# Splitting the blocks of U ahead of the V loop: an adding DMA for every second block, VectorE for the rest

## The chip, the core and the metric

One core of a Trainium2 chip. It has five engines, each with an instruction queue of its own that is worked off in order: TensorE (PE, with its weight loads PEld shown apart), VectorE (DVE), ScalarE (ACT), GpSimd (POOL) and SyncE (SP), which here only issues DMAs. SP's transfers are the hardware queue q1 in the profile, GpSimd's the software queue q0; both run on the same 16 DMA engines. The metric is the device time of one execution in microseconds (us).

## The reference, cut to what matters

A decoder layer for 512 tokens of width 1024: attention in two head groups, then PEER. PEER routes each token to 128 of 16384 single-neuron experts (8 heads, 16 each), and for the chosen ones computes

```python
expert = jnp.take_along_axis(cand_i, best_pos, axis=-1)
g = jax.nn.softmax(best_s, axis=-1)
act = jax.nn.gelu(jnp.einsum('cd,chkd->chk', hc, u[expert]), approximate=False)
out = jnp.einsum('chk,chkd->cd', g * act, v[expert])
```

## The kernel before, in words

For the first 384 tokens (three tiles of 128) PEER is done densely: U and V are cut into 128 blocks of 128 experts; all activations of a block are computed and multiplied by a gate matrix that is zero where an expert was not chosen. The last 128 tokens gather their rows of U and V by indirect DMA on GpSimd's queue instead.

Every float32 product is made of three matmuls on rounded halves: a matrix is split in a high part (`hi`, rounded) and a low part (`lo = raw - hi`), and `mm3` (lines 147 to 150) multiplies high by high, high by low and low by high. `u_block(b)` (line 875) does this for one block of U: SP loads 512 KB of float32 (`raw`, two buffers, L878), ScalarE writes `hi` (L881, three buffers), the low part is made in one of three ways (below, three buffers), then 24 matmuls (8 chunks of three; L148, L149, L150) fill one PSUM bank (`p_u`), and ScalarE takes the GELU of it (L892). The activations of the first 22 blocks are stored to DRAM by SP (`a_d`, two buffers, L894).

The low part is made

- by an adding DMA where `b in UDMA`: ScalarE writes the negated rounded copy into `lo` (L883), and GpSimd issues a DMA that reads the block from DRAM once more and adds it (L884);
- else by GpSimd where `b in UPOOL`, else by VectorE, as one subtraction of two tiles (L886).

`UDMA` is asked first, so that of `UPOOL`'s 14 numbers only 0 and 52 count; blocks 1, 2, 3, 53, 54 and 55 are VectorE's, and so are blocks 56 to 127.

```python
if b in UDMA:
    nc.scalar.activation(lo, raw, AF.Copy, scale=-1.0)
    nc.gpsimd.dma_start(lo.rearrange("p k e -> p (k e)"), ut[b], accum_op=ALU.add)
else:
    (nc.gpsimd if b in UPOOL else nc.vector).tensor_tensor(lo, raw, hi.bitcast(F32), op=ALU.subtract)
```

56 blocks (`NAHEAD`) are done ahead, while the gates are made. Routing (`route`: 8 largest values, replace, indices, all on VectorE), the choice of experts (`choose`: VectorE, with ScalarE's expanded copies `ix`, L776), `spread`, and then for each of the three token tiles eight steps: `hot` writes one-hot tables on VectorE (L823, L826, two buffers each), `gates` multiplies them on PE (32 small matmuls a step, `p_g`, L842), ScalarE copies the result (`st`, L845), and SP stores 1 MB (`g_d`, L848). After each step `u_ahead(2)` adds two blocks of U; six come before the first step and two after the last. Routing and choice for the next tiles are written between the steps of tiles 0 and 1. In the text the first gathers (`gu`, L918, on GpSimd's queue, with L926 on VectorE) stand in the second half of tile 2.

Then the loop over V (`v_load`, `v_mm`): per block two loads, two splittings, 18 matmuls (L1019), and one block of U for the later blocks, plus the gathers for the last 128 tokens.

The order of each engine's instructions is not the order of the text: a planner under the kernel runs the program against costs of its own and takes what is ready, the most urgent first. `tc.high_priority(offset=UPRI)` makes the load and splitting of a U block as urgent as text 1000 instructions earlier. The order it finds is then fixed, and on the chip every engine keeps to it.

Of the kernel before, what the change touches and what calls it, by code (L numbers as in the profile page):

```python
# [53 lines left out]
XAT = (0, 1)  # L54
UPRI = 1000
PACE = 1.02
UPOOL = tuple(range(0, 56, 4))
LAST = 4
UDMA = tuple(range(4, 52))
VRB = 3  # L60
ARB = 3
RATE = (0.2, 2.75, 1.1)
# [13 lines left out]
def hybrid_layer(ctx: ExitStack, tc, x, pos, wada, wada_n, cols, w_small, w_in_a, w_in_b, wuk, wuv,  # L76
# [798 lines left out]
    def u_block(b, psum):  # L875
        with tc.high_priority(offset=UPRI):
# [4 lines left out]
            nc.scalar.activation(hi, raw, AF.Copy)  # L881
# [5 lines that stand above are left out]
        o = psum(f"p_u{b}")[:, :DT]  # L887
# [247 lines left out]
```

## Time and profile before

| | us |
|---|---|
| median of 3 timed runs | 1613.36 (1611.5 to 1625.25) |
| the profiled execution | 1609.18 |
| its span, first to last instruction | 1607.1 |
| around the span | 2.1 |

The profile is of one execution. A window of it is named by microseconds from the start of the span. The attention part ends near 430 us, the gates and the blocks of U ahead take from there to about 760 us, and the loop over V and the end take the rest.

### The profile page before, as it was taken

The page shows a single profiled execution, that of the slowest core. Times are in us where ns is not written, and L with a number is a line of the kernel's source. Part 1 is how long each engine was busy: PE and PEld are TensorE (multiplying, and loading weights), DVE is VectorE, ACT ScalarE, POOL GpSimd, SP SyncE. Part 2 cuts the span into 40 slices and gives each one's busy share as a digit, 9 for nine tenths or more (in the row PEclk, how much of TensorE's full clock was granted, in tenths as well). Part 3 has the DMA queues.
Part 4 walks back from the last instruction along what each step waited for, and adds up shares of the span by engine and source line. Part 5 has one row for each costly group of instructions (what it writes and reads, how often), then busy time and mean ns, then how long its engine had stood idle before and what let it go on. Part 6 is the DMA issues. An engine that isn't in the chain of part 4 may idle for free.

```text
span 1607.1 us, 23098 instructions
## 1 busy us (share of the span) xinstructions
PE 1503.8 (94%) x8136; PEld 1319.1 (82%) x8138; DVE 1230.5 (77%) x2623; ACT 753.6 (47%) x1190; POOL 538.8 (34%) x439
## 2 busy tenths in 40 slices
PE   6888898999899888899999999999999999999997
PEld 5757687777788788789888999999999999998885
DVE  7698986856989798343567887888888888776886
ACT  4655446544268678586333333333333333333333
POOL 2323213112111222111003645554555555553420
PEclk7999899999999999999999999999999999999999
DMA  8233333513199999998987999999999999997974
GB/s 341 79 118 106 106 131 105 171 66 96 29 239 275 295 303 289 304 287 258 316 283 263 342 388 348 323 364 309 345 355 326 342 324 355 348 306 252 334 254 156
DMA packets 161733, 410.93 MB, mean 256 GB/s; under 512 B 12865, under 2 KB 69073, under 8 KB 158289
## 3 DMA queue, kind: packets, MB, share of 16 engines
q1 hardware_dynamic: 116832, 248.81, 45.6%
q0 software_dynamic: 43776, 159.40, 30.5%
q8 instruction: 64, 1.05, 0.3%
q10 hardware_dynamic: 1008, 1.24, 0.2%
q14 instruction: 53, 0.43, 0.1%
HBM read 375.71 MB, written 33.69 MB: 255 GB/s over the span
## 4 chain that ended last, share of the span: by engine, by line
PE 69%; DVE 10%; ACT 8%; DMA 7%; issue 5%; POOL 1%; DVEq 0%; POOLq 0%; ACTq 0%; SPq 0%
PE acc L1019 31%; PE p_u L150 8%; PE p_u L149 8%; PE p_u L148 8%; PE po L561 2%; DMA a_d<-a 2%; DMA ulo<-in_ut_dram 2%; ACT st L845 2%; PE p_g L842 1%; PE p_b L148 1%; PE tp L551 1%; ACT ulo L883 1%; PE pl L535 1%; PE p_b L150 1%; PE p_b L149 1%
## 5 line engine op out<-in xcount | busy, mean ns | idle before, releaser
L150 PE MATMUL p_u<-h,ulo 128*128 128x384 f32 x1024 | 349.0, 341 | 17.1 <-DMA ulo<-in_ut_dram 17.1
L148 PE MATMUL p_u<-h,uhi 128*128 128x384 f32 x1024 | 348.6, 340 | 3.0 <-ACT a L892 3.0
L149 PE MATMUL p_u<-h,uhi 128*128 128x384 f32 x1024 | 346.3, 338 | 0.0
L918 POOL DMA_INDIRECT gu<-in_un_dram,e x128 | 190.2, 1486 | 270.1 <-DVE gu L926 239.2
L881 ACT ACTIVATE uhi<-u 128x1024 fp32r<-128x1024 f32 x128 | 135.5, 1060 | 265.8 <-PE p_u L149 213.5
L918 POOL DMA_INDIRECT gv<-in_pv_dram,e x128 | 189.4, 1479 | 187.2 <-DVE acc L937 156.3
L1019 PE MATMUL acc<-vhi,wh 128*128 128x512 f32 x768 | 237.2, 389 | 0.6 <-ACT wh L1011 0.6
L1019 PE MATMUL acc<-vlo,wh 128*128 128x512 f32 x768 | 237.3, 389 | 0.0
L1019 PE MATMUL acc<-vhi,wl 128*128 128x512 f32 x768 | 237.1, 389 | 0.0
L150 PEld LDWEIGHTS p_u<-h,ulo 128*128 128x128 f32 x1024 | 193.7, 189 | 21.7 <-DMA ulo<-in_ut_dram 19.0
L1011 ACT ACTIVATE wh<-w 128x384 fp32r<-128x384 f32 x128 | 67.3, 525 | 302.8 <-issue 179.5
L148 PEld LDWEIGHTS p_u<-h,uhi 128*128 128x128 f32 x1024 | 193.8, 189 | 7.1 <-ACT a L892 4.0
L149 PEld LDWEIGHTS p_u<-h,uhi 128*128 128x128 f32 x1024 | 193.8, 189 | 2.9
L1012 DVE TENSOR_TENSOR wl<-w,wh 128x384 fp32r<-128x384 f32 x128 | 71.4, 558 | 136.6 <-ACT wh L1011 136.4
L926 DVE SCALAR_TENSOR_TENSOR gu<-gu,h2n 128x1024 f32<-128x1024 f32 x128 | 154.2, 1221 | 21.3 <-DMA gu<-in_un_dram,e 21.1
L1019 PEld LDWEIGHTS acc<-vlo,wh 128*128 128x128 f32 x768 | 144.0, 188 | 30.3 <-DVE vlo L998 0.4
L1019 PEld LDWEIGHTS acc<-vhi,wl 128*128 128x128 f32 x768 | 144.2, 188 | 30.1
L937 DVE SCALAR_TENSOR_TENSOR acc<-gv,w,acc 128x1024 f32<-128x1024 f32 x127 | 162.6, 1280 | 5.0 <-DMA gv<-in_pv_dram,e 4.9
L1019 PEld LDWEIGHTS acc<-vhi,wh 128*128 128x128 f32 x768 | 143.2, 188 | 25.4 <-ACT wh L1011 0.9
L998 DVE TENSOR_TENSOR vlo<-v,vhi 128x1024 fp32r<-128x1024 f32 x128 | 156.2, 1220 | 3.9 <-ACT vhi L997 3.8
L997 ACT ACTIVATE vhi<-v 128x1024 fp32r<-128x1024 f32 x128 | 135.5, 1058 | 10.3 <-PE acc L1019 4.3
L884 POOL DMA_DIRECT2D ulo<-in_ut_dram x48 | 42.5, 886 | 208.9 <-ACT ulo L883 202.4
(356 smaller groups left out, 2460.2 us busy)
## 6 DMA issues: line engine op xcount, KB each, us to landing
u<-in_ut_dram SPq DMA_DIRECT2D x128, 512.0 KB, 6.3
v<-in_pv_dram SPq DMA_DIRECT2D x128, 512.0 KB, 4.9
ulo<-in_ut_dram POOLq DMA_DIRECT2D x48, 512.0 KB, 8.3
g_d<-st SPq DMA_DIRECT2D x24, 1024.0 KB, 7.4
gt<-g_d SPq DMA_DIRECT2D x48, 512.0 KB, 8.5
wada<-in_wada_dram SPq DMA_DIRECT2D x32, 512.0 KB, 3.3
raw_b<-in_w_in_b_dram SPq DMA_DIRECT2D x12, 512.0 KB, 3.7
a_d<-a SPq DMA_DIRECT2D x22, 192.0 KB, 7.3
```

Of the source, the lines that this page charges most:

```text
L148: nc.tensor.matmul(o, ahi, bhi, start=start, stop=False, **kw)
L149: nc.tensor.matmul(o, ahi, blo, start=False, stop=False, **kw)
L150: nc.tensor.matmul(o, alo, bhi, start=False, stop=stop, **kw)
L881: nc.scalar.activation(hi, raw, AF.Copy)
L918: nc.gpsimd.indirect_dma_start(out=t, out_offset=None, in_=src, in_offset=bass.IndirectOffsetOnAxis(ap=e0[:, s:s + 1], axis=0))
L926: nc.vector.scalar_tensor_tensor(t, t, 1.0, h2n, op0=ALU.mult, op1=ALU.mult, accum_out=dot0[:, s:s + 1])
L937: nc.vector.scalar_tensor_tensor(acc0, t, w0[:, s:s + 1], acc0, op0=ALU.mult, op1=ALU.add)
L997: nc.scalar.activation(hi, raw, AF.Copy)
L998: nc.vector.tensor_tensor(lo, raw, hi.bitcast(F32), op=ALU.subtract)
L1011: nc.scalar.activation(wh, w, AF.Copy)
L1012: last[0] = nc.vector.tensor_tensor(wl, w, wh.bitcast(F32), op=ALU.subtract).ins
L1019: nc.tensor.matmul(accs[2 * j + n], l[:, js], r[:, n * 512:(n + 1) * 512], start=b == 0 and i == 0, stop=b == NK - 1 and i == 2)
```

## The change

The numbers of the blocks change hands; no instruction is new.

```diff
-UPOOL = tuple(range(0, 56, 4))
+UPOOL = ()
 LAST = 4
-UDMA = tuple(range(4, 52))
+UDMA = tuple(range(5, 53, 2))
```

The adding DMA keeps the 24 odd blocks from 5 to 51. The 24 even blocks from 4 to 50 go from it to VectorE, and so do blocks 0 and 52 from GpSimd.

## Rows read from the trace of the kernel before

**Rows 1.** The head of the page: span, and busy time with share of the span and number of instructions of each engine.

```profile
span 1607.1 us, 23098 instructions
...
PE 1503.8 (94%) x8136; PEld 1319.1 (82%) x8138; DVE 1230.5 (77%) x2623; ACT 753.6 (47%) x1190; POOL 538.8 (34%) x439
```

**Rows 2.** Busy time by stretch. Columns: stretch in us from the span's start, its length, then busy us (and number of instructions) of PE, of PE's weight loads, of VectorE, of ScalarE and of GpSimd, the granted clock of TensorE, the busy share of the DMA engines, GB/s. The seventh row is the whole of the first five and the 33 us before them; the last row is the loop over V.

```profile
480.00:530.00 50.00, 46.95 (x342) 43.78 (x342) 48.48 (x216) 40.87 (x48) 11.65 (x15) 1.00 0.97 278
530.00:545.00 15.00, 10.39 (x56) 9.46 (x54) 7.83 (x45) 4.85 (x7) 2.37 (x3) 0.77 1.05 315
545.00:585.00 40.00, 35.62 (x290) 32.66 (x289) 35.47 (x107) 36.85 (x45) 8.50 (x9) 1.00 1.01 303
585.00:640.00 55.00, 48.88 (x373) 45.01 (x372) 47.51 (x161) 45.56 (x55) 13.38 (x15) 1.00 0.98 278
640.00:690.00 50.00, 42.12 (x307) 38.68 (x306) 20.70 (x34) 30.86 (x39) 10.00 (x11) 0.97 1.00 291
690.00:745.00 55.00, 52.77 (x404) 50.83 (x403) 20.72 (x31) 42.04 (x51) 10.48 (x10) 1.00 1.01 295
...
447.00:690.00 243.00, 213.56 (x1525) 197.65 (x1524) 188.36 (x711) 181.45 (x219) 52.88 (x60) 0.98 0.99 281
...
870.00:1572.00 702.00, 702.00 (x3491) 632.54 (x3490) 576.91 (x725) 250.69 (x345) 353.75 (x236) 1.00 0.93 329
```

**Rows 3.** The same view for the instructions on the PSUM tile of the gate products (p_g) alone; columns: stretch, length, PE, ScalarE, clock, DMA share, GB/s.

```profile
447.00:690.00 243.00, 42.25 (x576) 67.59 (x72) 0.98 0.99 281
690.00:745.00 55.00, 10.84 (x160) 19.66 (x22) 1.00 1.01 295
```

**Rows 4.** The same for the U products (p_u); columns: stretch, length, PE, PE's weight loads, ScalarE, clock, DMA share, GB/s.

```profile
447.00:690.00 243.00, 179.55 (x913) 159.25 (x912) 18.54 (x38) 0.98 0.99 281
690.00:745.00 55.00, 44.64 (x244) 41.65 (x243) 4.72 (x10) 1.00 1.01 295
```

**Rows 5.** What PE waited for from 690 to 745 us. Columns: who waited, for whom, us in total, times, longest us.

```profile
PE p_g L842 <- ACT st L845: 2.2, 5, 0.5
```

**Rows 6.** The busy time by stretch for the score products of the routing (p_sc); columns: stretch, length, PE, weight loads, VectorE, clock, DMA share, GB/s.

```profile
447.00:690.00 243.00, 6.15 (x24) 4.22 (x24) 27.53 (x150) 0.98 0.99 281
```

**Rows 7.** What PE waited for from 447 to 690 us, columns as in rows 5.

```profile
PE p_u L150 <- DMA ulo<-in_ut_dram: 17.1, 11, 3.7
PE p_g L842 <- ACT st L845: 6.5, 11, 1.5
PE p_g L842 <- DVE oh L826: 3.5, 3, 1.4
PE p_u L148 <- ACT a L892: 1.7, 2, 0.9
```

**Rows 8.** The chain that ended last, from 505 to 550 us: start us, us, what.

```profile
522.46 9.86 DMA a_d<-a
...
532.92 10.02 DMA a_d<-a
```

**Rows 9.** ScalarE's wait for the store of the activations in the same stretch, columns as in rows 5.

```profile
ACT a L892 <- DMA a_d<-a: 12.5, 5, 5.0
```

**Rows 10.** VectorE's four longest waits in the same stretch, columns as in rows 5.

```profile
DVE o L811 <- ACT tt L805: 21.1, 2, 19.9
DVE oh L823 <- PE p_g L842: 11.4, 5, 7.2
DVE gu L926 <- DMA gu<-in_un_dram,e: 10.0, 3, 4.8
DVE eq L780 <- ACT ix L776: 8.0, 5, 2.6
```

**Rows 11.** The DMA view from 447 to 690 us: queue, packets, MB and the share of the 16 engines' time in the stretch; then issues: tile, queue, kind, number, KB each, median us from issue to landing.

```profile
q0 software_dynamic: 7390, 26.93, 51.2%
q1 hardware_dynamic: 10837, 41.20, 47.4%
...
ulo<-in_ut_dram POOLq DMA_DIRECT2D x39, 512.0 KB, 8.4
...
gu<-in_un_dram,e POOLq DMA_INDIRECT x13, 11.9
```

**Rows 12.** The GpSimd queue's row of the same view from 900 to 1400 us, where that queue issues gathers only.

```profile
q0 software_dynamic: 25983, 94.58, 50.3%
```

**Rows 13.** The instructions that write the low part (tile ulo), whole kernel. Columns: line, engine, kind, number, ns min/median/max, first and last start in us, shape.

```profile
L886 DVE TENSOR_TENSOR ulo<-u,uhi x78: 1207/1222/1229, 435.2 to 1433.5; 128x1024 fp32r<-128x1024 f32 x78
L883 ACT ACTIVATE ulo<-u x48: 1039/1043/1096, 445.6 to 736.1; 128x1024 fp32r<-128x1024 f32 x48
L884 POOL DMA_DIRECT2D ulo<-in_ut_dram x48: 854/858/1130, 447.0 to 737.5; - x48
L886 POOL TENSOR_TENSOR ulo<-u,uhi x2: 2342/2567/2792, 429.6 to 740.5; 128x1024 fp32r<-128x1024 f32 x2
```

**Rows 14.** The chain that ended last, in one even step of the last gates: start us, us, what.

```profile
718.49 1.03 ACT ulo L883
719.52 0.38 ACT a L892
719.89 0.95 ACT st L845
```

**Rows 15.** VectorE's wait for ScalarE before a low part, 690 to 780 us, columns as in rows 5.

```profile
DVE ulo L886 <- ACT uhi L881: 18.3, 6, 5.6
```

## The prediction, made before the changed kernel ran

> **What bounds the kernel now.** I read the head of the page first [rows 1]: PE is busy for 94% of the span, but that is a mean over stages with different limits. The table of stretches comes next [rows 2]. Its last row, the loop over V, has PE busy for all of 702 us: nothing that happens beside PE can shorten it, and it holds no block that the change touches. So the change is worth what it does between 430 and 760 us, where U ahead and the gates share the chip.
>
> In that stage two paces stand side by side. From 690 to 745 us the gates run evenly: 5 steps (160 gate matmuls at 32 a step [rows 3]) and 10.2 blocks of U (244 matmuls at 24 a block [rows 4]) in 55 us, 11.0 us a step, with PE waiting for 2.2 us [rows 5]. That is PE's own pace. From 447 to 690 us there are 38.0 blocks (913/24 [rows 4]) and 18 steps (576/32 [rows 3]), and 6.2 us of score products [rows 6]. At the even pace the blocks and steps would take 18 x 11.0 = 198 us and the two blocks over that some 8 us (PE needs 44.6/10.2 = 4.4 us a block [rows 4]); with the score products 212 us. They took 243. So some 31 us lie there, and no more: this is the ceiling of any gain in that stretch.
>
> Who holds PE there: the adding DMA 17.1 us, ScalarE's copies and GELUs 6.5 + 1.7 us, VectorE's tables 3.5 us [rows 7]; some 29 us. After such waits the granted clock is 0.77 of full speed from 530 to 545 us and 0.97 from 640 to 690 (a mean over its two levels, 2.4 and 1.2 GHz) [rows 2], which adds 0.23 x 15 + 0.03 x 50 = 5 us. And behind two of these waits stands the DMA too: the chain goes through two stores of activations of 9.9 and 10.0 us [rows 8], for which ScalarE stood for 12.5 us [rows 9], with its copies for the U blocks queued behind. The DMA engines are busy for 99% of the stretch, VectorE for 188.4 us of 243 [rows 2], with 54.6 us idle, nearly all in four waits [rows 10].
>
> **What the change takes from the DMA engines.** The GpSimd queue took 51.2% of 243 us, 124 us, for 39 adding DMAs and 13 gathers [rows 11]. What a gather costs alone is seen in the loop over V: 50.3% of 500 us for 94.6 MB, 2.66 us a MB [rows 12], 1.39 us for its 0.524 MB. 13 gathers are 18 us, so 39 adds are 106 us, 2.7 us each; a plain load on the hardware queue is 0.474 x 243/41.2 = 2.80 us a MB [rows 11], 1.5 us. Half of the adds, 20 in the stretch, free 20 x 2.7 = 54 us: the engines' load goes from 240 to about 186 us of 243, 77%.
>
> The Trainium skill ("DMA: Bandwidth & Descriptors", section "SDMA does more than copy") says that a DMA engine's arithmetic lies in line with the data stream, and gives no rate. Taken as a plain load's price, half the adds would free 29 us and leave the engines at 87%; the trace has 2.7 us for an add against 1.5, so the measurement decides, and the relief is the larger one.
>
> **What it takes from ScalarE and GpSimd.** 24 negated copies of 1.043 us and 24 issues of 0.858 us [rows 13], 25 and 21 us. In the even steps a negated copy stands ahead of the GELU and of the gate copy that PE waits for [rows 14]; one of two per step goes. Blocks 0 and 52: 2.34 and 2.79 us on GpSimd become 1.22 on VectorE [rows 13]; I take 0, with 1.6 us as the bound of either sign each, since VectorE is full at the first and PE has blocks in hand at the second.
>
> **What comes back to PE.** Half of the blocks lose the wait for the adding DMA (8.5 of 17.1 us); the other half's adds land sooner, and fewer of them stand between GpSimd's gathers. I take 11 us, between 8.5 and 17.1. Of the 8.2 us on ScalarE I take 4 (bounds 0 and 8.2), of the clock 3 (0 and 5), of the even steps 2 (0 and 2.2). Sum: 20 us off; all bounds together give 33, and the ceiling above with the even steps gives the same 33.
>
> **What it adds.** 26 subtractions of 1.222 us on VectorE [rows 13], 31.8 us; 20 of them in 447 to 690, 24.4 us against 54.6 us idle. But 21.1 us of that idle time is the start of a tile's gates, nearly all one wait of 19.9 us [rows 10] late in the stretch, which takes no work that is due earlier. From 480 to 640 VectorE is busy for 139.3 of 160 us [rows 2], and its share there, 12 subtractions, is 15 us into 20.7. Queued behind each of them stand the one-hot tables for PE's gate products and the routing of the next tile, and the block's `raw` buffer, so SP's next load, waits for it as well. PE meanwhile has U blocks to do. I take 9 us as lost: between 0 (PE always has another block) and 25.6 (20 in the stretch and one in the full VectorE before it, each delaying PE by its length). Half-way down, because VectorE is full in one part of the stretch (97% from 480 to 530) and not in the other. No price is in the trace for the new order that the planner will find; it acts through the same waits, and I leave it inside these bounds.
>
> So the stage gets shorter by 20 - 9 = 11 us: 1598 us against the profiled 1609.2, which lies 4 us below the median; on the median's footing **1602 us**. By its terms' likelier ends this case runs from 4 to 19 us off, 1594 to 1609.
>
> **Rivals.**
> 1. The whole relief. The subtractions fit into VectorE's idle time because the waits for gathers (10.0 us) and for PE (11.4 us) [rows 10], which slow DMAs and a late PE cause, go. Then 25 us off (19 to 33): 1588. For it: the DMA engines at 99%, and 54.6 us idle against 24.4. Against it: VectorE at 97% from 480 to 530.
> 2. VectorE becomes the bound of tiles 0 and 1. All 25.6 us show: -20 + 25.6 = +5, no change to be measured, 1619. For it: 139.3 of 160 us. Against: PE doesn't depend on the gates alone, it has U blocks as well.
> 3. Slower, by one mechanism: VectorE's queue is in order, and a subtraction waits there for `hi`, which ScalarE writes when PE gives a buffer back. VectorE, which could run ahead of PE until now, is then tied to it. Where such waits are seen, they are 18.3/6 = 3.05 us [rows 15]. 20 of these are 61 us; with 24.4 of work 85.4 against 54.6 idle: 31 us slower, 1644. It decides from (54.6 - 24.4)/20 = 1.5 us a subtraction; at 2.3 us it costs the 16 us that are 1%. For it: the planner's times are not the chip's. Against: the six waits lie where VectorE has nothing else to do, and three buffers of `hi` leave two blocks, 8 us, of lead.
>
> **How the numbers follow.** Forecast 0.48, rival 1 0.22, rival 2 0.17, rival 3 0.13. A measurement tells about 1%, 16 us, from no change. Faster by more: rival 1 and the forecast's far end, 0.30. Slower by more: most of rival 3, 0.09. Within: 0.61. Range 1586 (27 us off, some 0.07 beyond) to 1623 (10 us more, some 0.12 beyond). Both signs hold chance; the likeliest case's own range is 1594 to 1609.
>
> **What would show it.** Right: 24 negated copies and 24 adds, 104 subtractions on VectorE and none on GpSimd; the DMA share between 447 and 690 near 0.8; PE's wait for the adding DMA under 7 us; the stores of activations landing in well under 9.9 us and ScalarE's wait for them under 4; the loop over V as long as before, beginning some 11 us earlier; VectorE over 93% busy from 480 to 640. Wrong: PE's waits for VectorE's tables or low parts of more than 10 us (rival 2), waits of VectorE for `hi` of more than 1.5 us a block (rival 3), or a DMA share still at 0.99.

## The result and the profile after

The changed kernel took 1602.83 us in the median of 12 runs, the kernel before 1620.69 in its 12 runs. The ratio on record, which is not the quotient of these two medians (0.9890), is 0.9912 with a 95% interval of 0.9885 to 0.9940, some 14 us of 1613 (10 to 19). The profiled execution took 1602.78 us. Its head, beside [rows 1]:

```profile
span 1600.3 us, 23058 instructions
...
PE 1501.5 (94%) x8136; PEld 1318.7 (82%) x8138; DVE 1257.0 (79%) x2649; ACT 731.7 (46%) x1166; POOL 516.6 (32%) x413
```

VectorE is 26.5 us busier, ScalarE 21.9 and GpSimd 22.2 less. The low parts, beside [rows 13]:

```profile
L886 DVE TENSOR_TENSOR ulo<-u,uhi x104: 1205/1218/1289, 435.8 to 1424.7; 128x1024 fp32r<-128x1024 f32 x104
L883 ACT ACTIVATE ulo<-u x24: 1037/1041/1078, 451.7 to 726.0; 128x1024 fp32r<-128x1024 f32 x24
L884 POOL DMA_DIRECT2D ulo<-in_ut_dram x24: 864/871/1134, 453.4 to 727.3; - x24
```

The table of stretches, columns and order as in [rows 2] (the whole stretch from 447 to 690 us first); the last row is the loop over V, which now begins some 10 us earlier:

```profile
447.00:690.00 243.00, 223.78 (x1617) 210.70 (x1615) 219.16 (x770) 173.70 (x211) 37.75 (x41) 0.98 0.85 256
480.00:530.00 50.00, 47.44 (x347) 44.49 (x346) 47.98 (x185) 37.69 (x46) 4.16 (x6) 1.00 0.79 233
530.00:545.00 15.00, 12.53 (x64) 12.21 (x63) 13.14 (x68) 6.40 (x9) 5.79 (x7) 0.89 1.02 346
545.00:585.00 40.00, 37.57 (x294) 34.78 (x293) 36.41 (x117) 34.63 (x42) 4.48 (x5) 1.00 0.80 230
585.00:640.00 55.00, 51.82 (x405) 48.89 (x404) 52.47 (x177) 41.87 (x51) 7.41 (x9) 1.00 0.84 263
640.00:690.00 50.00, 43.59 (x349) 40.22 (x347) 37.84 (x63) 34.63 (x43) 12.36 (x11) 0.97 0.95 303
690.00:745.00 55.00, 52.16 (x401) 50.26 (x401) 22.84 (x32) 36.49 (x45) 3.52 (x4) 1.00 0.78 235
860.00:1562.00 702.00, 701.88 (x3490) 632.24 (x3489) 576.70 (x726) 250.06 (x343) 355.88 (x236) 1.00 0.93 329
```

The reader is to see three things. The loop over V is as full as before: nothing came from there. The DMA engines fell from 99% to 85% of the stretch. And VectorE was filled where it had idled: 37.8 of 50 us from 640 to 690 (20.7 before), and from 480 to 640 the four rows add up to 150.0 of 160 (139.3 before). PE paid little for it: its wait for VectorE's tables grew from 3.5 to 7.8 us. What PE waited for from 447 to 690 us, beside [rows 7]:

```profile
PE p_g L842 <- DVE oh L826: 7.8, 11, 1.4
PE p_u L150 <- DMA ulo<-in_ut_dram: 7.7, 3, 3.2
PE p_g L842 <- ACT st L845: 3.4, 6, 1.0
```

VectorE's waits there, beside [rows 10]; the waits of 21.1 us for `tt` and 11.4 us for PE's gates are gone:

```profile
DVE ulo L886 <- ACT uhi L881: 15.1, 11, 4.0
DVE gu L926 <- DMA gu<-in_un_dram,e: 6.6, 2, 3.8
DVE eq L780 <- ACT ix L776: 1.3, 2, 1.1
```

The DMA view of the stretch, beside [rows 11]. ScalarE's wait for `a_d`, 12.5 us in [rows 9], has no row any more:

```profile
q1 hardware_dynamic: 11536, 44.57, 53.6%
q0 software_dynamic: 4738, 17.28, 30.8%
...
ulo<-in_ut_dram POOLq DMA_DIRECT2D x20, 512.0 KB, 7.9
a_d<-a SPq DMA_DIRECT2D x21, 192.0 KB, 5.8
gu<-in_un_dram,e POOLq DMA_INDIRECT x13, 9.0
```

**The stage as one account.** From ScalarE's last copy of `qT` to PE's first product of the loop over V (L1019) PE has the same work in both kernels, 2175 rows. So the stage's length is PE's busy time plus its waits (a microsecond or so lies in gaps that no wait is listed for). The same table, the kernel before first:

```profile
427.93:775.23 347.30, 309.12 (x2175) 289.79 (x2175) 237.88 (x863) 246.10 (x297) 67.52 (x73) 0.98 0.95 275
```

and the changed kernel:

```profile
430.35:764.85 334.50, 306.75 (x2175) 290.32 (x2175) 264.42 (x890) 224.49 (x272) 42.02 (x47) 0.97 0.82 248
```

12.8 us less, of 14 in the timed runs. PE's clock has two levels, 2.4 and 1.2 GHz, and the waits do not show what the lower one costs. In the changed kernel the lower one was granted from 462.15 to 465.57 us, just behind a wait of 2.1 us for an adding DMA; columns as in [rows 2]:

```profile
462.15:465.57 3.42, 3.42 (x13) 3.42 (x12) 3.39 (x31) 0.89 (x2) 0.10 (x1) 0.50 0.86 206
```

The products of U in it start every 0.32 us, and those behind it every 0.17 (start us, us, what):

```profile
464.26 0.53 PE L150 MATMUL p_u<-h,ulo 128*128 128x384 f32 x1
464.58 0.53 PE L148 MATMUL p_u<-h,uhi 128*128 128x384 f32 x1
...
467.30 0.33 PE L149 MATMUL p_u<-h,uhi 128*128 128x384 f32 x1
467.47 0.33 PE L150 MATMUL p_u<-h,ulo 128*128 128x384 f32 x1
```

So the stretch at 1.2 GHz costs 0.15 of each 0.32 us that PE is busy in it. The waits over this stage, the time in it that PE was busy at 1.2 GHz, and the same of every kernel run later (us; "adds" are adding DMAs in the stage; the last column but one is an estimate, the stage less 0.15/0.32 of the column before it; the timed ratio is against the kernel before):

| kernel | adds | stage | PE <- adding DMA | PE <- ScalarE (`st`, `a`) | PE <- VectorE's tables | PE busy at 1.2 GHz | stage without its cost | timed ratio |
|---|---|---|---|---|---|---|---|---|
| before | 48 | 347.3 | 17.1 | 12.3 | 3.5 | 12.1 | 342 | 1 |
| changed | 24 | 334.5 | 7.7 | 7.5 | 7.8 | 14.0 | 328 | 0.9912 |
| e1_plain_even | 24 and 24 plain | 345.1 | 12.3 | 13.4 | 3.5 | 18.4 | 336 | 0.9971 |
| e2_upool_only | 48 | 351.4 | 18.1 | 11.9 | 3.5 | 22.1 | 341 | 0.9995 |
| e3_udma_only | 24 | 343.6 | 13.4 | 7.7 | 7.5 | 13.1 | 337 | 0.9978 |
| e4_act_copy | 24 | 340.9 | 10.6 | 9.8 | 6.2 | 16.0 | 333 | 0.9957 |
| e5_no_low | 24 | 355.5 | 0.8 | 32.0 | 3.6 | 27.6 | 343 | 1.0028 |
| e6_dve_and_dma | 48 | 353.6 | 16.6 | 12.7 | 4.1 | 23.1 | 343 | 1.0032 |
| e7_pool0 | 24 | 337.9 | 8.5 | 10.3 | 5.5 | 19.1 | 329 | 0.9944 |
| e8_tile0_dma | 33 | 344.9 | 14.3 | 10.3 | 6.3 | 16.2 | 337 | 0.9980 |
| e9_short_sub | 24 | 341.0 | 9.4 | 7.6 | 10.4 | 16.7 | 333 | 0.9953 |
| e10_double_sub | 24 | 335.9 | 8.8 | 12.3 | 5.5 | 10.6 | 331 | 0.9946 |
| e11_all_dve | 0 | 327.6 | 0 | 7.1 | 8.9 | 10.7 | 323 | 0.9880 |
| e12_third | 32 | 345.8 | 11.5 | 13.1 | 3.3 | 27.8 | 333 | 0.9993 |

The stage's difference over 1609 us agrees with each timed ratio within 0.3%, so the stage carries the effect as far as these times can tell; 0.3% is some 5 us, a third of it. (The span doesn't serve: the last copy of `qT`, ahead of all that is changed, lay anywhere from 428 to 440 us in the profiled executions, and what follows the stage took 831.9 us before, 835.5 in the changed kernel and 832.6 to 836.2 in the others. So the two profiled executions as wholes are only 6.4 us apart.) Each row is of one execution, and how much the stage varies from one execution to the next was not measured.

With the estimated cost of 1.2 GHz taken out the stages fall into an order that the plain lengths hide: 341 to 343 us for the three kernels with 48 adds, 328 to 333 with 24 and VectorE on the other blocks, 323 without any.

### The profile page after: what moved, and what is told of

It reads as the page before. It is cut to its first block, busy times and chain, and to the rows that moved or that the text cites. A ratio compares the mean times of both kernels' runs of the same rounds, so it can differ in the third digit from the quotient of the medians.

```text
span 1600.3 us, 23058 instructions
## 1 busy us (share of the span) xinstructions
PE 1501.5 (94%) x8136; PEld 1318.7 (82%) x8138; DVE 1257.0 (79%) x2649; ACT 731.7 (46%) x1166; POOL 516.6 (32%) x413
## 4 chain that ended last, share of the span: by engine, by line
PE 64%; DVE 10%; ACT 6%; issue 5%; DMA 4%; POOL 1%; SPq 0%; DVEq 0%; POOLq 0%; ACTq 0%
PE acc L1019 28%; PE p_u L150 8%; PE p_u L148 8%; PE p_u L149 8%; ACT st L845 2%; PE po L561 2%; DMA gu<-in_un_dram,e 1%; DMA ulo<-in_ut_dram 1%; DVE ulo L886 1%; PE p_g L842 1%; ACT uhi L881 1%; PE pl L535 1%; PE tp L551 1%; PE p_b L148 1%; PE p_b L149 1%
## 5 line engine op out<-in xcount | busy, mean ns | idle before, releaser
L918 POOL DMA_INDIRECT gv<-in_pv_dram,e x128 | 193.9, 1515 | 181.4 <-DVE acc L937 148.9
L1019 PE MATMUL acc<-vlo,wh 128*128 128x512 f32 x768 | 237.3, 389 | 0.9 <-DVE vlo L998 0.9
L1019 PE MATMUL acc<-vhi,wh 128*128 128x512 f32 x768 | 237.4, 390 | 0.4 <-ACT wh L1011 0.2
L1019 PE MATMUL acc<-vhi,wl 128*128 128x512 f32 x768 | 237.1, 389 | 0.0
L886 DVE TENSOR_TENSOR ulo<-u,uhi 128x1024 fp32r<-128x1024 f32 x104 | 126.9, 1220 | 63.9 <-ACT uhi L881 63.6
L1019 PEld LDWEIGHTS acc<-vlo,wh 128*128 128x128 f32 x768 | 144.0, 188 | 31.4 <-DVE vlo L998 1.6
L1019 PEld LDWEIGHTS acc<-vhi,wl 128*128 128x128 f32 x768 | 144.1, 188 | 30.1
L1019 PEld LDWEIGHTS acc<-vhi,wh 128*128 128x128 f32 x768 | 143.1, 188 | 25.6 <-ACT wh L1011 1.0
```

Of the source, the lines that this page charges most:

```text
L918: nc.gpsimd.indirect_dma_start(out=t, out_offset=None, in_=src, in_offset=bass.IndirectOffsetOnAxis(ap=e0[:, s:s + 1], axis=0))
L1019: nc.tensor.matmul(accs[2 * j + n], l[:, js], r[:, n * 512:(n + 1) * 512], start=b == 0 and i == 0, stop=b == NK - 1 and i == 2)
```

## The experiments

All were timed against the kernel before. The theory was that of the prediction: the DMA engines' relief and ScalarE's give, VectorE's subtractions cost. Nearly every edit makes the planner find a new order; e1 is the exception, there every engine keeps the order of before (e2 comes near it). The diffs of e1, e2, e3 and e6 are against the kernel before, the others against the changed one.

**e1_plain_even.** The DMA engines' arithmetic alone.

```diff
-    nc.gpsimd.dma_start(..., ut[b], accum_op=ALU.add)
+    nc.gpsimd.dma_start(..., ut[b], **(dict(accum_op=ALU.add) if b % 2 else {}))
```

> The kernel before, but for the even blocks 4 to 50 the DMA that adds is a plain DMA of the same bytes on the same queue (the low part is then the raw block; that part of the computation is wrong). The order of every engine's instructions is the same as before, and nothing else changes: only the price of 24 transfers, 2.7 us of the DMA engines by the trace, falls to that of a plain one, some 1.5. My theory (the gain is relief of the DMA engines): 24 x 1.2 = 29 us of DMA time go, about half of what the change frees, so 6 to 12 us faster than before (ratio 0.992 to 0.996), PE's wait for the adding DMA from 17 to 10 us or less, ScalarE's wait for the stores of activations from 12.5 to under 8. Rival A (the gain is ScalarE's relief from the negated copies) and rival B (the gain is the planner's new order): no change, 0.999 to 1.001.

Measured: ratio 0.9971 (0.9944 to 0.9997), some 5 us, short of the expected 0.992 to 0.996, which the interval reaches; it leaves out 1, though only just. PE's wait for the adding DMA fell from 17.1 to 12.3 us and ScalarE's for the stores of activations from 12.5 to 10.3, both less than expected. The two main queues from 447 to 690 us, as in [rows 11]:

```profile
q1 hardware_dynamic: 11134, 42.50, 50.1%
q0 software_dynamic: 7488, 27.27, 41.9%
```

Nearly the same bytes (27.27 MB, 26.93 before) took 41.9% and not 51.2% of the engines. 41.9% of 243 us less 18 for the gathers is 84 us for 39 transfers; with half of them adds of 2.7 us, a plain one comes to 1.6 us. The Trainium skill ("DMA: Bandwidth & Descriptors", section "SDMA does more than copy") places the arithmetic in line with the stream and gives no rate; on this queue the same 512 KB cost 1.1 us more with it. So the price of an add in the prediction holds, and arithmetic is the smaller part of the gain, some 5 of 14 us: the block still waits for its DMA.

**e2_upool_only.** Blocks 0 and 52 alone.

```diff
-UPOOL = tuple(range(0, 56, 4))
+UPOOL = ()
```

> One part of the change alone: blocks 0 and 52 go from GpSimd to VectorE, the adding DMA keeps blocks 4 to 51. My prediction took 0 for this part, with 1.6 us per block as the bound of either sign: ratio 0.998 to 1.002. Rival from the trace after: at the start VectorE is full, the low part of block 0 waits in its queue, the raw buffer comes free 5 us later and with it the next load, so PE begins the blocks 2 to 4 us later: 1.001 to 1.0025, and the third load of U is issued near 437 us in place of 432.

Measured: 0.9995 (0.9968 to 1.0021). The term of 0 holds within this interval, which does not exclude the lower half of the rival's range: the next load of U was issued at 437.5 us and not at 432.0, and the one stage that was profiled is 4.1 us longer.

**e3_udma_only.** The other line alone. With the even blocks out of `UDMA`, `UPOOL` counts again and GpSimd makes the low part of 14 blocks (0, 4, 8 to 52).

```diff
-UDMA = tuple(range(4, 52))
+UDMA = tuple(range(5, 53, 2))
```

> The other part alone: the adding DMA keeps the odd blocks 5 to 51, and GpSimd keeps its list, so that blocks 0, 4, 8 to 52 are subtracted on GpSimd (14, of 2.6 us each), the other even ones on VectorE. If VectorE's added work is what is lost (my 9 us), half of it comes back: 3 to 6 us faster than the change (ratio to before 0.986 to 0.990), VectorE busy for some 140 us of 480 to 640 in place of 150. Rival: the subtractions on GpSimd hold up the adds and gathers behind them on its queue and take twice as long: slower than the change, 0.993 to 1.000, with PE's wait for low parts above 12 us.

Measured: 0.9978 (0.9955 to 1.0001), the rival's range. So the empty `UPOOL` is not idle text: most of the gain hangs on it, 0.22% being left of 0.88. The stage is 9.1 us longer than the changed kernel's. PE's wait for the adding DMA is 5.7 us more of that, and 3.9 us are waits for the transposes of `spread` (`tp_s`, L803) behind VectorE, which the changed kernel does not have. One thing that stands ahead of these transposes is seen in the trace. GpSimd's longest subtraction (the median is 2.45 us), columns start us, us, what:

```profile
574.75 6.26 POOL L886 TENSOR_TENSOR ulo<-u,uhi 128x1024 fp32r<-128x1024 f32 x1 [3.77 <-ACT uhi L881]
```

and VectorE beside it:

```profile
578.33 0.29 DVE L782 TENSOR_TENSOR eq<-eq 128x256 f16<-128x256 f16 x1
578.53 0.23 DVE L796 CAST i<-sel 128x128 int32<-128x128 f32 x1
578.67 2.43 DVE L782 TENSOR_TENSOR eq<-eq 128x128 f16<-128x128 f16 x1
```

GpSimd stands while VectorE runs eight two-input operations in a row, until these break off at a CAST; then VectorE's next one, half the size of one of 0.29 us, takes 2.43 us and ends as GpSimd ends, at 581.0. Each holds the other up. The Trainium skill ("SBUF — State Buffer", section "SBUF: two separate sides") says that the two share a pair of ports as an exclusive lock for a whole instruction; these rows agree, on both sides. Of the 14 subtractions only one other was held up by more than half a microsecond (4.00 us). So this accounts for a few us, and why the adds were waited for longer, by the lock, by GpSimd's queue or by the planner's order, is not shown.

**e4_act_copy.** The changed kernel with ScalarE's relief taken back.

```diff
 else:
+    if b in range(4, 52):
+        nc.scalar.activation(lo, raw, AF.Copy, scale=-1.0)
     (nc.gpsimd if b in UPOOL else nc.vector).tensor_tensor(lo, raw, ...)
```

> The change, with the 24 negated copies on ScalarE kept for the even blocks (VectorE writes over them), so ScalarE is as loaded as before. My theory: ScalarE's relief is worth 4 of the 20 us, so 2 to 6 us slower than the change, ratio to before 0.992 to 0.996. Rival A (the gain is ScalarE's relief): the gain is gone, 0.998 to 1.002.

Measured: 0.9957 (0.9932 to 0.9982), in the range of the theory. That is 7 us slower than the changed kernel by the two ratios, whose intervals just overlap; PE's waits for ScalarE 9.8 us in place of 7.5. The subtraction here waits for the copy as well (10.4 us in VectorE's list), so 7 us is rather more than what the copies cost.

**e5_no_low.** Meant to show VectorE's cost by taking the subtractions away.

```diff
+    elif b in range(4, 52):
+        lo = hi
```

> The changed kernel, but the 24 even blocks from 4 to 50 get no low part: their products take the high part twice, so those 24 numbers of the output are wrong and VectorE's 24 subtractions (24 x 1.22 us) are gone; loads, ScalarE, the 24 adds and PE's work stay. Theory (the subtractions cost some 9 us because VectorE is full in tile 0 and not in tile 1): 5 to 13 us faster than the changed kernel, ratio to the kernel before 0.983 to 0.988, and the gain lies in the first eight steps of the gates (before 82.7 us, changed 85.3, here under 80), VectorE from 480 to 640 us well under 140 us busy. Rival a (the subtractions fit into idle time): as the changed kernel, 0.990 to 0.993. Rival b (VectorE is the bound of tiles 0 and 1 and shows all): 20 us or more faster than the changed kernel, under 0.979.

Measured: 1.0028 (0.9998 to 1.0059), no faster than the kernel before; all three expectations missed. PE's longest wait, over the stage:

```profile
PE p_g L842 <- ACT st L845: 29.9, 20, 6.8
```

and ScalarE's:

```profile
ACT ulo L883 <- DMA u<-in_ut_dram: 39.1, 17, 6.3
```

The odd blocks' negated copies now stand in ScalarE's queue ahead of their loads' landing, with `st` behind them; probably because the buffers of the even low parts were never written and came free earlier for the planner. The run says nothing of VectorE's cost. It says that one bad order costs more than the change is worth: its stage is 21 us longer than the changed kernel's.

**e6_dve_and_dma.** VectorE's load and ScalarE's relief, without the DMA's.

```diff
-    nc.scalar.activation(lo, raw, AF.Copy, scale=-1.0)
+    if b % 2:
+        nc.scalar.activation(lo, raw, AF.Copy, scale=-1.0)
+    else:
+        nc.vector.tensor_tensor(lo, raw, hi.bitcast(F32), op=ALU.subtract)
     nc.gpsimd.dma_start(..., ut[b], accum_op=ALU.add)
```

> The kernel before, but in the 24 even blocks VectorE's subtraction takes the place of ScalarE's negated copy and the adding DMA still runs on top of it (so the low parts of these blocks are wrong). VectorE's load and ScalarE's relief are those of the changed kernel; the load of the DMA engines and GpSimd's issues are those of the kernel before. Theory (ScalarE's relief is worth some 7 us, the subtractions cost some 9, the DMA's relief is kept out): ratio 0.998 to 1.006, DMA share from 447 to 690 us 0.97 or more, PE's wait for the adding DMA 15 us or more. Rival (the gain comes from ScalarE's copies and the planner's new order, not from the DMA engines): 0.988 to 0.995.

Measured: 1.0032 (0.9999 to 1.0066), with PE's wait for the adding DMA at 16.6 us: as the theory had it. Without the DMA's relief there is no gain, so neither ScalarE's copies nor moving the subtractions to VectorE makes it alone, in this order at least. The run is no clean exchange: an even block's DMA here waits for VectorE's subtraction ahead of it, and VectorE waited for `hi` ahead of these subtractions for 46.6 us in the stage.

**e7_pool0 and e8_tile0_dma.** Two attempts at a better split: block 0 back on GpSimd, then also blocks 4 to 21 back on the adding DMA.

```diff
-UPOOL = ()
+UPOOL = (0,)
-UDMA = tuple(range(5, 53, 2))
+UDMA = tuple(range(4, 22)) + tuple(range(23, 53, 2))    # e8 alone
```

> The changed kernel with block 0's low part back on GpSimd (block 52 stays on VectorE). In the changed kernel block 0's low part began 6 us later (435.8 against 429.6 us) and the third load of U was issued at 437 instead of 432 us. Theory (that start costs what it shows, 2 to 4 us): ratio 0.987 to 0.990, with the load back at 432 us. Rival (PE has score products and the planner other work in hand there, VectorE is the bound of what follows): as the changed kernel, 0.990 to 0.993.

> The changed kernel with block 0 on GpSimd as in the run before this, and with all blocks from 4 to 21 (those done up to the end of the first eight steps of the gates) back on the adding DMA; from 22 on, even blocks on VectorE and odd ones on the DMA as in the changed kernel. Theory (VectorE is full in the first eight steps and gains nothing there from the DMA's relief; the whole gain is that of the next eight steps): the first eight steps back to some 82 us, the next eight stay at some 73 to 78, in all 2 to 6 us faster than the changed kernel, ratio 0.986 to 0.990. Rival (the gain of the second eight steps was prepared by the relief in the first, whose stores and loads then lie earlier): the second eight steps go back to 85 us or more and the ratio to 0.994 to 0.999.

Measured: 0.9944 (0.9919 to 0.9970) and 0.9980 (0.9953 to 1.0008). Neither theory held; e8's ratio lies in its rival's range. In e7 the load went out at 434.0 us (437.0 in the changed kernel, 432.0 before) and nothing came of it. In e8 PE's wait for the adding DMA was 14.3 us, and the second eight steps, 72.8 us in the changed kernel, took 83.4 (93.1 before), from the eighth store of gates to the sixteenth. I had read the gain of those steps as theirs alone, because the first eight had become 2.6 us longer; e8 speaks for its being prepared in part by the relief in the first, though its order is another too.

**e9_short_sub and e10_double_sub.** VectorE's cost again, with the buffers in use: subtractions an eighth as long, then each made twice.

```diff
-    (nc.gpsimd if b in UPOOL else nc.vector).tensor_tensor(lo, raw, hi.bitcast(F32), op=ALU.subtract)
+    n = 1 if b in range(4, 52) else KC
+    nc.vector.tensor_tensor(lo[:, :n], raw[:, :n], hi[:, :n].bitcast(F32), op=ALU.subtract)
...
-    mm3(o, hi[:, k], lo[:, k], ...)
+    mm3(o, hi[:, k], lo[:, 0 if b % 2 == 0 and 4 <= b < 52 else k], ...)    # e9
```

```diff
     (nc.gpsimd if b in UPOOL else nc.vector).tensor_tensor(lo, raw, hi.bitcast(F32), op=ALU.subtract)
+    if b in range(4, 52):
+        nc.vector.tensor_tensor(lo, raw, hi.bitcast(F32), op=ALU.subtract)    # e10
```

> The changed kernel, but in the 24 even blocks from 4 to 50 VectorE makes only the first of the eight chunks of the low part, and the products take that chunk for all eight (their numbers are wrong). Buffers, who writes and who reads stay as in the changed kernel; 24 subtractions of 1.22 us become an eighth as long. Unlike the run without any low part, no buffer of the low part stays unused, so ScalarE's copies for the next odd block cannot be put ahead of their load. Theory (in the changed kernel the subtractions cost PE the 4 us that its wait for one-hot tables grew, 3.5 to 7.8, and little more): PE's wait for those tables in the stage back under 5 us, 2 to 8 us faster than the changed kernel, ratio 0.986 to 0.990. Rival (the planner's order decides more than VectorE's 26 us): 0.994 or more, with a wait in PE's list that neither kernel had. Rival (9 us or more, as predicted): 0.985 or less.

> The changed kernel with every subtraction of the 24 even blocks from 4 to 50 made twice: 29 us more on VectorE, nothing else. From 447 to 690 us VectorE was busy for 219 of 243 us in the changed kernel, so the 20 or so that lie there, 24 us, just fill it. Theory (VectorE had room for one subtraction per two blocks, not for two): it becomes the bound of the first two tiles, 12 to 28 us slower than the changed kernel, ratio 0.999 to 1.009, PE's waits for VectorE (tables and low parts) over 15 us. Rival (PE has U blocks to do meanwhile and nothing shows): 0.989 to 0.995.

Measured: 0.9953 (0.9920 to 0.9985) for the shorter, 0.9946 (0.9916 to 0.9975) for the doubled ones. Both lie in rivals' ranges, e9 in that of the planner's order. The shorter ones took 0.27 us, 23 us less in all, and helped nothing; PE's list had no new wait either, its wait for tables even came to 10.4 us. 29 us more hardly hindered: the stage grew by 1.4 us. e10 from 447 to 690 us, columns as in [rows 2]:

```profile
447.00:690.00 243.00, 225.32 (x1589) 214.26 (x1588) 228.56 (x754) 168.94 (x205) 37.04 (x40) 0.99 0.84 244
```

and PE's waits for VectorE in it:

```profile
PE p_g L842 <- DVE oh L826: 5.5, 9, 1.2
```

VectorE is at 94%, and PE waits no more for it than in the changed kernel. The gate products and the U products by stretch (as in [rows 3, 4]) say how. The changed kernel, first the gates, then U:

```profile
530.00:690.00 160.00, 33.57 (x480) 58.12 (x60) 0.98 0.88 275
690.00:765.00 75.00, 10.85 (x160) 19.16 (x21) 1.00 0.81 255
...
530.00:690.00 160.00, 118.04 (x610) 107.26 (x608) 12.75 (x26) 0.98 0.88 275
690.00:765.00 75.00, 62.31 (x343) 58.73 (x342) 6.61 (x14) 1.00 0.81 255
```

and e10:

```profile
530.00:690.00 160.00, 28.71 (x414) 51.41 (x52) 0.99 0.85 253
690.00:765.00 75.00, 19.30 (x256) 30.57 (x32) 0.98 0.88 296
...
530.00:690.00 160.00, 124.15 (x655) 114.19 (x655) 13.75 (x28) 0.99 0.85 253
690.00:765.00 75.00, 50.70 (x265) 45.34 (x264) 5.38 (x11) 0.98 0.88 296
```

With VectorE late, PE does 45 more U products and 66 fewer gate products from 530 to 690 us, and then makes up for the gates in tile 2, where VectorE had been idle for more than half of the time.

**e11_all_dve and e12_third.** The step once more, and two thirds of it.

```diff
-UDMA = tuple(range(5, 53, 2))
+UDMA = ()                                              # e11
+UDMA = tuple(b for b in range(4, 52) if b % 3)         # e12
```

> The same step once more: the odd blocks' adds go to VectorE too, so that there is no adding DMA and no negated copy at all. VectorE gets 24 more subtractions (29 us), ScalarE loses 25 us of copies, the DMA engines lose 24 x 2.7 us. Theory (what was to be had of the DMA is had: PE waits for it for 7.7 us only, and VectorE is full): slower than the changed kernel by 3 to 16 us, ratio 0.994 to 1.002. Rival (the DMA and ScalarE give as much for the second half as for the first): 0.980 to 0.988.

> Two thirds of the change: of the blocks 4 to 51 every third goes to VectorE (16 subtractions), 32 keep the adding DMA; blocks 0 and 52 on VectorE. Theory (the DMA engines' relief and the wait for the adding DMA go with the number of adds): between the kernel before and the changed one, 0.993 to 0.997, DMA share from 447 to 690 us 0.88 to 0.93, PE's wait for the adding DMA 9 to 13 us. Rival (the DMA is relieved once it is off its full load, and VectorE has less to do): 0.987 to 0.992. Rival (an order with every second block is what counts, not the number): 0.998 or more.

Measured: 0.9880 (0.9839 to 0.9921, 6 runs) without any add, 0.9993 (0.9964 to 1.0021) with 32. My theory for e11 (slower than the changed kernel) is refuted; its rival had it. e11's stretch:

```profile
447.00:690.00 243.00, 230.24 (x1659) 218.77 (x1658) 234.25 (x764) 154.82 (x190) 20.12 (x17) 0.99 0.60 205
```

and PE's waits in it:

```profile
PE p_g L842 <- DVE oh L826: 7.9, 11, 1.8
PE tp_s L803 <- DVE sel L783: 3.0, 1, 3.0
PE p_g L842 <- ACT st L845: 1.8, 4, 0.6
```

VectorE at 96%, the DMA engines at 60%, no wait for a DMA, and the stage 20 us shorter than before. That is the best stage of all; its interval overlaps that of the changed kernel, so that it beats it is likely and not shown. e12 missed its expectation on the low side and lies in the range of its second rival, that an order with every second block is what counts and not the number: 16 blocks fewer on the DMA gave nothing that can be measured. The trace speaks for another cause. Its wait for the adding DMA did fall as expected (11.5 us) and the DMA share too (0.88), but PE was busy for 312.7 us with the same products (306.8 in the changed kernel), 27.8 of them at 1.2 GHz, where the kernel before had 12.1 and the changed one 14.0. Without that cost its stage comes to 333 us, as long as those of the slower kernels with 24 adds. The mean clock of its 12 runs was the lower one as well, 0.9725 against 0.9746 in the runs of the kernel before beside them. By this estimate the number of adds does count; what pulled the clock down in e12 was not tried.

## Why the prediction was right, and where its steps were not

The forecast was a stage 11 us shorter and 1602 us, with 4 to 19 us for the likeliest case. 12.8 us came in the stage and some 14 in the timed runs. That the median is 1602.83 is chance: the forecast went from a kernel before of 1613 us, and in the runs beside the changed kernel that one took 1620.69. Term by term, over the whole stage:

- **The wait for the adding DMA.** Predicted 11 (8.5 to 17.1); measured 17.1 - 7.7 = 9.4. The DMA share came to 0.85 where 0.77 was worked out, and 6 of these 8 points are the hardware queue's (53.6% against 47.4): 4 because it moved 44.6 MB in the stretch (41.2 before), as the stage ran faster, and 2 because a MB took the engines 2.92 us in place of 2.80. The sign that was named beforehand, a wait under 7 us, was missed by 0.7.
- **ScalarE.** Predicted 4; PE's waits for `st` and `a` fell from 12.3 to 7.5, by 4.8. e4 gives up to 7.
- **The clock.** Predicted 3; measured none. The granted clock from 530 to 545 us was 0.89 (0.77 before), but PE was busy at 1.2 GHz for 14.0 us of the stage and not for 12.1. PE's busy time for the same rows fell all the same, by 309.1 - 306.8 = 2.4 us; what that is, no run shows.
- **The even steps.** Predicted 2; measured none. PE's wait there stayed:

```profile
PE p_g L842 <- ACT st L845: 2.8, 5, 0.6
```

and the chain of the changed kernel passes the gates every 11.04 us (before: 709.99 to 731.78 us for two steps, 10.90):

```profile
709.62 0.62 PE p_g L842 x8
...
720.66 0.62 PE p_g L842 x8
...
731.70 0.62 PE p_g L842 x8
```

The copy that I took off the path of the even steps [rows 14] was not what set their pace; PE, busy for 52.2 of the 55 us, was.
- **VectorE.** Predicted 9 lost (0 to 25.6); measured 7.8 - 3.5 = 4.3 more waiting for tables. With PE's shorter busy time these terms sum to 9.4 + 4.8 + 2.4 - 4.3 = 12.3 of the 12.8 us.
- **Blocks 0 and 52, the loop over V, the stores.** As predicted: nothing (e2), 701.9 of 702 us busy, `a_d` landing in 5.8 us (a median of 7.3 before) with ScalarE's wait for it gone.

So the mechanism came as forecast, but the sum is as near as it is by luck: what I let come back was some 6 us too much (20 against 14.2), what I took as lost 5 us too much (9 against 4.3), and 2.4 us came from where I had nothing.

The step that failed by its reasoning is VectorE's. I wrote that its idle time before a tile's gates "takes no work that is due earlier". It does: VectorE, with four of the subtractions and other work pushed back there from earlier, came to the tables of the last tile at 665 us and not at 655, ScalarE's `tt` was there at 659 and not at 675, and the 21.1 us wait is gone. And I charged PE for VectorE's delays, 9 of 25.6 us, though I named the reason against it under rival 2, that PE has U blocks to do. e10 and e11 show that it is the main thing: VectorE at 94 and 96% of the stretch, PE waiting for 5.5 and 10.9 us. Rival 2 is thus out, and not only for this number of subtractions. Rival 3 did not come: VectorE's waits for `hi` were 15.1 us for 21 subtractions from 447 to 690 us, 0.72 each, half of the 1.5 from which it was to decide. (Another 44.1 us of them lie after 690 us, where VectorE has little else to do.) Rival 1 (25 us off, 19 to 33) was right that the subtractions find room because waits of VectorE go. Of the two waits it named in [rows 10] the one for PE (11.4 us) went and the one for gathers only fell from 10.0 to 6.6; the one for `tt`, which it did not name, went too. The whole relief, 14 us or 17 with PE's shorter busy time, stayed under what it supposed.

**What is not settled.** I left the planner's order "inside these bounds". Five kernels with the same 24 adds and VectorE on the rest of these blocks (the changed one, e4, e7, e9, e10) have stages of 334.5 to 341.0 us and ratios of 0.9912 to 0.9957, mean 0.9942. Three of them were given work that should make them slower or faster (e4, e10, e9), and still the changed kernel is the best of the five. So some 7 to 9 us are what the division of the blocks is worth in each of these orders, and the last 5 or so may be a lucky order or a lucky execution; the intervals, about 0.3% each way, don't separate the two. With 48, 33, 32, 24 and 0 adds the plain stages are 347.3, 344.9, 345.8, 334.5 and 327.6 us; with the cost of 1.2 GHz taken out, by the estimate above, they come down more evenly: 342, 337, 333, 328 and 323. How the gain divides between less time on the DMA engines and one wait less in a block's chain is not shown; only the arithmetic's part was tried alone (e1). Nor is it shown how far the time at 1.2 GHz, which can follow a wait of PE's, belongs to the division itself.

## What to carry to other kernels

The transfer that computes was charged twice here, with the engines' time and with a wait in the middle of a block's chain; moving such a one to an engine that looks full can pay, if the engine that sets the end has other work to do while that one is late. Before charging a busy engine's added work to the time, ask who waits for it, and whether it can do something else first. Where a planner fixes the order, an experiment that changes buffers or lengths changes the order too: account for the bound engine's busy time, its clock and its waits over a stage with constant work, and trust a small difference only when several orders agree.

## What the runs showed of the hardware that was not expected

- A DMA of 512 KB on GpSimd's queue took the 16 engines some 2.7 us with an addition (kernel before) and 1.6 us without (e1), worked out from that queue's share of a stretch.
- A subtraction of 128x1024 on GpSimd, 2.35 us when undisturbed, took 6.26 us in one case beside VectorE, and there held a VectorE operation of some 0.2 us for 2.43 us (e3).
